# A seven-product MLP in fp32r: partial sums stay in PSUM banks that ScalarE saves and restores, split weights in one ring, and 34 of 64 half steps instead of 30 in seven products

## The chip, the core and the metric

The kernel runs on one core of one Trainium2 chip, in one launch. The metric is the device time of one execution in microseconds (us); the median of several runs is given with the lowest and the highest. Engines are named as the profile names them: PE (TensorE matmuls), PEld (its weight loads), DVE (VectorE), ACT (ScalarE), POOL (GpSimd), SP (the queue that issues the DMAs).

## What is computed

One layer of a hybrid decoder: 256 tokens, width 2048, everything in float32. An input projection feeds a state-space group and a sparse-attention group, an output projection brings both back, and an MLP follows. The change touches the MLP alone, the last two lines:

```python
    x = x + jnp.concatenate([y_ssd, y_att], axis=-1) @ w_out

    u = rmsnorm(x, g_mlp) @ w_up
    return x + jnp.square(jax.nn.relu(u)) @ w_down
```

`w_up` is 2048 x 8192 and `w_down` 8192 x 2048, 67 MB each. The "second MLP product" is the one with `w_down`.

## The kernel before

**Split numbers.** Every operand of the large products is split into a high and a low part of type fp32r: ACT casts the raw weights to the high part (L155), and DVE subtracts that from the raw weights, which leaves the low part (L156). A product of two such operands takes three matmuls (`three`, L195 to L203): high by high (L200), low by high (L202) and high by low (L203). In the MLP the row factor of the RMSNorm is left out ahead of the products. Since the ReLU is squared, it comes back as its square, `rs4`, in the additions to the residual `xr`.

**The stages.** The width 8192 of the MLP is cut into 32 pairs of 256 columns. They fall into three parts h = 0, 1, 2 of 10, 11 and 11 pairs (PARTS, L48). Each part has an up stage (`up`, L918) that makes the activations of its pairs, transposed, squared and split (`uh`, `ul`), and a down stage (`down`, L977) that multiplies them with the rows of `w_down`. A down stage has two halves, j = 0 and 1, one for each 1024 output columns. A pair in a half is called a half step here: 2 x 32 = 64 in all. PE goes through them in the order in which the code is written (PE's order is by hand, the other engines' order comes from the scheduler, which takes weights early through `high_priority`).

**A half step.** It multiplies a 2 x 2 block matrix of activations (two blocks of 128 tokens by two of 128 hidden columns) with a 2 x 2 block matrix of weights (128 rows by 512 columns each). The plain form has eight block products of `three`, 24 matmuls of 128x512. The form with seven products, in the manner of Strassen and Winograd, has seven, 21 matmuls. It needs sums of weight blocks: two additions of width 1024 (L966) and 512 (L969, two) on DVE, then casts and subtractions of the seven operands in two tiles: `wb` for three of them (L964, L974), `w2m` for the four sums (L967, L970, L974). SEVEN (L49) names the pairs in seven products: 0, 2, 4, 6, 8 in each half, 30 half steps of the 64. Below, such a half step is called S and a plain one P.

**Where sums lie.** PSUM has two sets of four banks of 128x512, tags "acc" and "mid". A half uses one set for its four output blocks (`acc`) and the other for four products of the seven that go into several output blocks (`ps7`). The other three products are added straight into `acc`. At the end of each half ACT copies the four product banks into a tile `m` (L1026), DVE combines them (L1027 to L1029), and DVE adds them (L997, through L993) and the four `acc` banks (L993) to the residual `xr`, times `rs4`. That happens in all six halves.

**Weights.** Each half step's weights, 1 MB, come with one DMA into a tile `rawm` (three of them) and are split into a `w2m` tile (three of them too). For S the sums go into `t`. So a half step's split can start as soon as a tile is free.

**CUTS (L45).** At the entry to a stage some matmuls are cut into two pieces at fixed columns (`three`, argument `cut`; the up stages have FIRST_W for it). They are the same matmuls in two pieces.

**The tail.** In the last half (h = 2, j = 1) the last two plain half steps are kept back and multiplied block by block, so that each output block of 512 columns is finished, added and stored while PE works on the next. The last block is cut into two halves of 256 columns.

## Time and profile before

| | |
|---|---|
| median of 3 runs | 1051.79 us (1051.16 to 1052.95) |
| the profiled execution, its own time | 1050.78 us |
| its span, first to last instruction | 1049.0 us |
| PE busy | 1043.5 us, 99% |
| weight loads busy | 927.1 us, 88% |
| DVE busy | 828.8 us, 79% |
| ACT busy | 565.4 us, 54% |
| granted clock of PE | 1.00 |

A row of the page gives a line of the kernel, the engine, the operation, out<-in by the program's names, the shape and how many there are; after the bar the sum of busy time and the mean of one in ns; after the second bar how long the engine stood idle just before these, and whose work ended that. A row of a timeline gives start and duration in us. Matmuls overlap, so the sum of their durations is more than the time that they take: their pace is the distance between their starts.

### The profile page before, as it was taken

The numbers are of one execution on the slowest core, as the hardware profiler recorded it, in microseconds if no ns is written. First come the engines' busy times: TensorE is split into PE (matmuls) and PEld (weight loads), VectorE is DVE, ScalarE is ACT, GpSimd is POOL, SyncE is SP. The second block draws the span as 40 slices with busy tenths as digits, with TensorE's granted clock in tenths as the row PEclk, the third lists the DMA queues.
The fourth block names the chain that finished last, engine by engine and source line by source line (L and its number), as shares of the span: only waits on it lengthen the run. The fifth ranks groups of instructions, "written<-read, shape, count | busy, mean of one in ns | idle before, by whom it ended". The sixth has DMA issues, their size and how long they took to land.

```text
span 1049.0 us, 14877 instructions
## 1 busy us (share of the span) xinstructions
PE 1043.5 (99%) x5926; PEld 927.1 (88%) x5926; DVE 828.8 (79%) x1035; ACT 565.4 (54%) x686; POOL 25.1 (2%) x30
## 2 busy tenths in 40 slices
PE   9999999999999999999999999999999999999998
PEld 8999999888888889888888898898888889888887
DVE  6698999577866557669899876688897866698996
ACT  6756555556665445445555544456545444555543
POOL 0020000122000000000000000000000000000000
PEclk9999999999999999999999999999999999999999
DMA  9957436544465536554665655555656555546671
GB/s 305 311 194 232 158 108 212 194 156 134 141 222 196 184 141 236 189 202 177 226 210 206 217 191 201 198 197 201 241 176 230 197 201 201 201 174 227 210 236 76
DMA packets 45317, 207.35 MB, mean 198 GB/s; under 512 B 4928, under 2 KB 9792, under 8 KB 29120
## 3 DMA queue, kind: packets, MB, share of 16 engines
q1 hardware_dynamic: 44960, 206.14, 57.9%
q8 instruction: 46, 0.75, 0.3%
q10 hardware_dynamic: 288, 0.26, 0.1%
q14 instruction: 23, 0.19, 0.1%
HBM read 204.29 MB, written 2.10 MB: 197 GB/s over the span
## 4 chain that ended last, share of the span: by engine, by line
PE 99%; DMA 1%; ACT 0%; DVE 0%; SPq 0%; issue 0%
PE acc L243 33%; PE acc L200 17%; PE acc L203 17%; PE acc L202 17%; PE acc L220 11%; DMA raw<-in_w_in 1%; PE ps_y L690 1%; PE ps_sr L774 0%; PE ps_l L728 0%; PE ps_o L753 0%; PE ps_s L580 0%; PE ps_s L581 0%; PE ps_dec L681 0%; PE ps_pt L745 0%; PE ps_yo L696 0%; PE pt_q L446 0%
## 5 line engine op out<-in xcount | busy, mean ns | idle before, releaser
L243 PE MATMUL acc<-x2x,w2m 128*128 128x256 f32 (+2 forms) x1987 | 331.5, 327 | 0.0
L243 PEld LDWEIGHTS acc<-x2x,w2m 128*128 128x128 f32 x1987 | 298.0, 188 | 33.2
L156 DVE TENSOR_TENSOR w2m<-rawm,w2m 128x2048 fp32r<-128x2048 f32 x96 | 219.5, 2288 | 49.2 <-ACT w2m L155 49.2
L155 ACT CAST w2m<-rawm 128x2048 fp32r<-128x2048 f32 x96 | 182.8, 1904 | 60.8 <-PE acc L203 35.6
L156 DVE TENSOR_TENSOR w<-raw,w 128x1024 fp32r<-128x1024 f32 (+1 forms) x116 | 140.2, 1214 | 71.2 <-ACT w L155 70.7
L155 ACT CAST w<-raw 128x1024 fp32r<-128x1024 f32 (+1 forms) x116 | 117.3, 1022 | 89.0 <-PE acc L203 63.6
L200 PE MATMUL acc<-w2m,uh 128*128 128x512 f32 (+3 forms) x405 | 150.2, 374 | 0.0
L203 PE MATMUL acc<-w2m,uh 128*128 128x512 f32 (+1 forms) x396 | 149.7, 378 | 0.0
L202 PE MATMUL acc<-w2m,ul 128*128 128x512 f32 (+1 forms) x396 | 149.7, 378 | 0.0
L220 PE MATMUL acc<-hx,w 128*128 128x256 f32 (+1 forms) x976 | 114.7, 278 | 0.0
L220 PEld LDWEIGHTS acc<-hx,w 128*128 128x128 f32 x976 | 112.6, 188 | 0.0
L927 ACT COPY r<-acc 128x256 f32<-128x256 f32 x64 | 23.3, 370 | 121.9 <-PE acc L243 121.3
L200 PEld LDWEIGHTS acc<-w2m,uh 128*128 128x128 f32 x405 | 76.0, 188 | 12.9
L202 PEld LDWEIGHTS acc<-w2m,ul 128*128 128x128 f32 x396 | 74.4, 188 | 12.3
L203 PEld LDWEIGHTS acc<-w2m,uh 128*128 128x128 f32 x396 | 74.3, 188 | 12.3
L967 ACT CAST w2m<-t 128x1024 fp32r<-128x1024 f32 x30 | 31.5, 1050 | 96.1 <-DVE t L966 40.7
L200 PE MATMUL acc<-w,hx 128*128 128x512 f32 (+3 forms) x226 | 82.6, 368 | 0.6 <-ACT w L356 0.6
L202 PE MATMUL acc<-w,hx 128*128 128x512 f32 (+1 forms) x222 | 79.8, 359 | 0.0
L203 PE MATMUL acc<-w,hx 128*128 128x512 f32 (+1 forms) x222 | 79.7, 359 | 0.0
L974 DVE TENSOR_TENSOR w2m<-t,w2m 128x2048 fp32r<-128x2048 f32 x30 | 68.6, 2287 | 12.7 <-ACT w2m L970 12.7
L974 DVE TENSOR_TENSOR wb<-rawm,wb 128x1536 fp32r<-128x1536 f32 x30 | 52.6, 1752 | 5.9 <-ACT wb L964 5.8
L928 DVE TENSOR_TENSOR r<-r,acc 128x256 f32<-128x256 f32 x64 | 26.4, 417 | 37.7 <-ACT r L927 37.7
(246 smaller groups left out, 1272.2 us busy)
## 6 DMA issues: line engine op xcount, KB each, us to landing
rawm<-in_w_down SPq DMA_DIRECT2D x64, 1024.0 KB, 4.8
rawm<-in_w_up SPq DMA_DIRECT2D x62, 1024.0 KB, 4.8
raw<-in_w_in SPq DMA_DIRECT2D x72, 512.0 KB, 3.9
raw<-in_w_out SPq DMA_DIRECT2D x32, 512.0 KB, 3.9
raw<-in_w_in SPq DMA_DIRECT2D x15, 256.0 KB, 5.2
raw<-in_w_in SPq DMA_DIRECT2D x16, 152.0 KB, 4.4
raw<-in_w_in SPq DMA_DIRECT2D x8, 304.0 KB, 3.3
xrow<-in_xn SPq DMA_DIRECT2D x4, 512.0 KB, 6.3
```

The lines of the kernel that those rows point to most:

```text
L155: nc.scalar.copy(hi[:, s], raw[:, s, :n])
L156: nc.vector.tensor_tensor(lo[:, s], raw[:, s, :n], hi[:, s].bitcast(F32), op=OP.subtract)
L200: nc.tensor.matmul(go(out[:, i:j]), ah, go(wh[:, i:j]), start=first and i == 0, stop=False, skip_group_check=True)
L202: nc.tensor.matmul(go(out), al, go(wh), start=False, stop=False, skip_group_check=True)
L203: nc.tensor.matmul(go(out), ah, go(wl), start=False, stop=last, skip_group_check=True)
L220: nc.tensor.matmul(acc[:, c, at:at + n], w[:, 0, s], x[:, fr:fr + n], start=(i + k + j == 0), stop=(i >= 2 and k == 7 and j == len(todo) - ...
L243: nc.tensor.matmul(walk(out[:, fr:fr + m]), w[:, k], walk(x[:, fr:fr + m]), start=(at + k + j == 0), stop=(at + k == KT - 1 and j == len(t ...
L690: nc.tensor.matmul(pt[:, 64 * i:64 * i + 64], m[i // 4][:, i % 4, :], xdt[:, c, 64 * h:64 * h + 64], start=True, stop=True)
L927: nc.scalar.copy(r[:, c], acc[:, T:])
L928: nc.vector.tensor_tensor(r[:, c], r[:, c], acc[:, :T], op=OP.add)
L967: nc.scalar.copy(ht[:, :2], t[:, :2])
L974: nc.vector.tensor_tensor(lo, x, hi.bitcast(F32), op=OP.subtract)
```

## The change

**Parts and half steps.** PARTS is (0, 11, 22, 32): parts of 11, 11 and 10 pairs. Instead of sets of pairs there is, for each half, a string of S and P (STEPS) in the order in which PE takes them; the pairs are assigned to the letters in turn, so that a pair that is S in one half is S in the other. Six S in each half of h = 0 and h = 1, five in each of h = 2: 34 half steps in seven products. The last half ends S S P P, and before it ended P S P P.

**Banks.** The sums are no longer finished at the end of each half. Between two halves ACT copies the four `ps7` banks into a tile `carry`, or the four `acc` banks into `xr`, and writes the banks' next contents into PSUM: the state of the other half's columns, from `xr` or from `carry` (`seed_acc`, `seed_p`, `save_acc`, interleaved by `exchange`). Matmuls then add to what the banks hold, without a start flag. The residual itself goes in at h = 0, multiplied by `mean2`, the inverse of `rs4`, and the factor `rs4` is applied by ACT as the bank is saved for the last time. The recombination of the four products (`solve`, `combine`) is done once for each j, in h = 2. The additions of the `acc` banks on DVE are left only in the last half.

**Weights.** The split weights of the MLP lie in one ring of 16 units of 512 columns, high parts in its first half and low parts in its second (RING). An S takes seven units, a P four, a column block of `w_up` four (it waits for five). A unit is free as soon as its last product is written down, not when the whole half step is done. The tiles `wb`, `t` and the three `w2m` are gone; the sums of weights are made in place in `rawm`. The order of the four blocks of `w_down` in memory is changed to fit that (`_quarters`). The low parts of the four sums are made in two instructions of 1024 columns where there was one of 2048, and a P that follows an S is split in two steps of two blocks (`cuts`). Where the units taken wrap around the ring's end, one more instruction is needed.

**Order.** ACT and DVE are now ordered by hand in the MLP as well: for each product on PE one step of the preparation of later weights is written down (`prepare`, as far ahead as the ring allows) and one instruction of an exchange (`lazy`).

The core of the diff:

```diff
-PARTS = (0, 10, 21, 32)
-SEVEN = (({0,2,4,6,8},{0,2,4,6,8}),({0,2,4,6,8},{0,2,4,6,8}),({0,2,4,6,8},{0,2,4,6,8}))
+PARTS = (0, 11, 22, 32)
+STEPS = (("SPSPSSPSSPP", "PSSPSPSSPSP"), ("SPSPSSPSSPP", "PSSPSPSSPSP"), ("SPSSPSPSPP", "PSSPSPSSPP"))
+TAGS = (("mid", "acc"), ("acc", "mid"), ("mid", "acc"))
+UP = ("acc", "mid", "acc")
+RING = 16
 
 A11, A21, A12, A22 = range(4)
 S1, S2, S4 = 4, 5, 6
-S3 = {7: 1, 8: 7}
-E, G, P1, F, M6 = range(5)
+S3 = 1
+P1, M6, E, F = range(4)
...
+    ring = mlp.tile([P, 2 * RING * 512 + SPARE], F32R, name="w2m")
...
+    def take(n):
+
+        if wide[0]:
+            wide[0] = False
+            head[0] += 1
+        units = [(head[0] + i) % RING for i in range(n)]
+        while any(busy[q] for q in units):
+            yield False
+        for q in units:
+            busy[q] = True
+        head[0] = (head[0] + n) % RING
+        return units
...
+    def plain(src, cuts):
+
+        with tc.high_priority(offset=HP):
+            raw = load(src, 512)
+        units = yield from take(4)
+        n = 4 // cuts
+        for i in range(0, 4, n):
+            with tc.high_priority(offset=HP):
+                for hi, lo, x in view(units[i:i + n], raw[:, i:i + n]):
+                    nc.scalar.copy(hi, x)
+                    nc.vector.tensor_tensor(lo, x, hi.bitcast(F32), op=OP.subtract)
+            if i + n < 4:
+                yield True
+        w22, w11, w21, w12 = (part(q) for q in units)
         return [[w11, w12], [w21, w22]]
...
-    def seven(src, behind):
+    def seven(src):
 
...
+            raw = load(src, 512)
+        own = yield from take(3)
+        with tc.high_priority(offset=HP):
+            for hi, lo, x in view(own, raw):
+                nc.scalar.copy(hi, x)
+                nc.vector.tensor_tensor(lo, x, hi.bitcast(F32), op=OP.subtract)
+        yield True
+        sums = yield from take(4)
+        outer, inner = (list(view(sums[2 * i:2 * i + 2], x)) for i, x in enumerate((raw[:, ::3], raw[:, 1:3])))
+        with tc.high_priority(offset=HP):
+            nc.vector.tensor_tensor(raw[:, ::3], raw[:, :2], raw[:, 3:].to_broadcast([P, 2, 512]), op=OP.add)
+            for hi, lo, x in outer:
+                nc.scalar.copy(hi, x)
+        yield True
+        with tc.high_priority(offset=HP):
+            for i in range(1, 3):
+                nc.vector.tensor_tensor(raw[:, i], raw[:, i], raw[:, i - 1], op=OP.add)
+            for hi, lo, x in outer:
+                nc.vector.tensor_tensor(lo, x, hi.bitcast(F32), op=OP.subtract)
+            for hi, lo, x in inner:
+                nc.scalar.copy(hi, x)
+        yield True
+        with tc.high_priority(offset=HP):
+            for hi, lo, x in inner:
+                nc.vector.tensor_tensor(lo, x, hi.bitcast(F32), op=OP.subtract)
+        return [part(own[i]) for i in (1, 2, 0)] + [part(sums[i]) for i in (1, 0, 2, 3)]
...
+    def seed_acc(h, j, i):
+
+        b, c = divmod(i, 2)
+        t = accumulator(TAGS[h][j])
+        state.setdefault((h, j), [[], []])[0].append(t)
+        src = xr[:, b, 1024 * j + 512 * c:1024 * j + 512 * c + 512]
+        if (h, j) == (2, 1):
+            return
+        if h:
+            nc.scalar.copy(t, src)
+        else:
+            nc.scalar.activation(t, src, AF.Copy, scale=mean2[:, b:b + 1])
+
+    def seed_p(h, j, i):
+
+        state.setdefault((h, j), [[], []])
+        t = accumulator(TAGS[h][1 - j])
+        state[h, j][1].append(t)
+        if h:
+            nc.scalar.copy(t, carry[:, 4 * j + (P1, F, E, M6)[i]])
+
+    def save_acc(h, j, i):
+
+        b, c = divmod(i, 2)
+        dst = xr[:, b, 1024 * j + 512 * c:1024 * j + 512 * c + 512]
+        if h + j == 2:
+            nc.scalar.activation(dst, state[h, j][0][i], AF.Copy, scale=rs4[:, b:b + 1])
+        else:
+            nc.scalar.copy(dst, state[h, j][0][i])
...
+        if g == 5:
+            for i in range(4):
+                seed_acc(h, 0, i)
...
+    def exchange(saves, seeds):
+
+        for i in range(5):
+            lazy.extend(saves[i:i + 1] + seeds[i - 1:i] if i else saves[:1])
...
+    def down_body(h, j, t, w):
+
...
+        if marked:
+            b11, b21, b22, t1, t3, t2, t4 = w
+            first = t == min(i for i, s in enumerate(steps) if s[1])
+            done = t == max(i for i, s in enumerate(steps) if s[1])
+            new = first and not h
+            p1, p5, p7, p6 = ps7
+            for n, (to, slot, right) in enumerate(((acc[0], A12, b21), (acc[1], S4, b22), (acc[2], A22, t4), (p1, A11, b11),
+                                                   (p5, S1, t1), (p7, S3, t3), (p6, S2, t2))):
+                go(to, x, slot, right, new if n > 2 else n not in opened, done and n > 2)
+                opened.add(n)
+                free(right[2])
+                if done and n == 6:
+                    exchange([lambda i=i: nc.scalar.copy(carry[:, 4 * j + (P1, F, E, M6)[i]], ps7[i]) for i in range(4)],
+                             [lambda i=i: seed_acc(h, 1, i) for i in range(4)] if j == 0 else [])
+                    if h == 2:
+                        solve(j)
...
+            turn = [(2 * b + c, k) for k in range(2) for c in range(2) for b in range(NB)]
+            for i, k in sorted(turn) if final else turn:
+                b, c = divmod(i, 2)
+                go(acc[i], x, 2 * k + b, w[k][c], i not in opened, final and k == 1)
+                opened.add(i)
+                if b:
+                    free(w[k][c][2])
+                if final and (i, k) == (3, 1):
+                    exchange([lambda i=i: save_acc(h, j, i) for i in range(4)],
+                             [lambda i=i: seed_p(h, 1, i) for i in range(4)] if j == 0 else [])
+                    if (h, j) == (2, 0):
+                        combine(0)
+                        lazy.append(lambda: [nc.sync.dma_start(out[b * P:(b + 1) * P, :1024], xr[:, b, :1024])
+                                             for b in range(NB)])
+                yield
...
+    for h in range(3):
+        for g in range(PARTS[h + 1] - PARTS[h]):
+            tag = "mid" if (h, g) in ((0, 1), (0, 3)) else UP[h]
+            for c in range(2) if h + g else ():
+                todo.append((lambda g=g, h=h, c=c: up_weights(w_up[PARTS[h] + g][c]),
+                             lambda w, h=h, g=g, c=c, tag=tag: up_body(h, g, c, w, accumulator(tag))))
+        for j in range(2):
+            for t, (g, marked) in enumerate(order[h, j]):
+                src = w_down[j, PARTS[h] + g]
+                cuts = 2 if t and order[h, j][t - 1][1] else 1
+                todo.append((lambda src=src, marked=marked, cuts=cuts: seven(src) if marked else plain(src, cuts),
+                             lambda w, h=h, j=j, t=t: down_body(h, j, t, w)))
...
+                    moved = next(task)
+                except StopIteration as e:
+                    ready.append(e.value)
+                    break
+                if not moved:
+                    yield
...
+    with tc.manual_schedule(engines={nc.scalar.engine, nc.vector.engine}):
+        prep = prepare()
+        next(prep, None)
+        for c in range(2):
+            up_rest(0, 0, c, first[c])
+        for i, (_, body) in enumerate(todo):
+            for _ in body(ready[i]):
+                if lazy:
+                    lazy.pop(0)()
+                next(prep, None)
...
-    w = np.stack([w[:, k, :, :, c] for k, c in ((0, 1), (0, 0), (1, 0), (1, 1))], axis=3)
+    w = np.stack([w[:, k, :, :, c] for k, c in ((1, 1), (0, 0), (1, 0), (0, 1))], axis=3)
```

Two places in the order of the instructions. First DVE in the first half of the down stage h = 0, before. `wb` and `w2m` are split weights, `t` sums of weights, `rawm` weights as they were loaded:

```order
L974 TENSOR_TENSOR wb<-rawm,wb 128x1536
L966 TENSOR_TENSOR t<-rawm 128x1024
L156 TENSOR_TENSOR w2m<-rawm,w2m 128x2048
L969 TENSOR_TENSOR t<-t,rawm 128x512 x2
L974 TENSOR_TENSOR w2m<-t,w2m 128x2048
L974 TENSOR_TENSOR wb<-rawm,wb 128x1536
L966 TENSOR_TENSOR t<-rawm 128x1024
L156 TENSOR_TENSOR w2m<-rawm,w2m 128x2048
```

The piece holds S, P, S and the beginning of the next: a P (one L156) stands between the first sum (L966) of an S and its second sums (L969). The same engine in the same half, after:

```order
L998 TENSOR_TENSOR w2m<-rawm,w2m 128x1024 x2
L1012 TENSOR_TENSOR w2m<-rawm,w2m 128x1536
L1017 TENSOR_TENSOR rawm<-rawm 128x2x512
L1023 TENSOR_TENSOR rawm<-rawm 128x512 x2
L1025 TENSOR_TENSOR w2m<-rawm,w2m 128x1024
L1031 TENSOR_TENSOR w2m<-rawm,w2m 128x1024
L1012 TENSOR_TENSOR w2m<-rawm,w2m 128x1536
L1017 TENSOR_TENSOR rawm<-rawm 128x2x512
L1023 TENSOR_TENSOR rawm<-rawm 128x512 x2
L1025 TENSOR_TENSOR w2m<-rawm,w2m 128x1024
L1031 TENSOR_TENSOR w2m<-rawm,w2m 128x1024
L998 TENSOR_TENSOR w2m<-rawm,w2m 128x1024 x2
```

Here two S follow each other (L1012 to L1031, twice), each with six instructions for its sums and splits, and a P cut in two (L998 x2) stands ahead and behind: P S S P, where S and P took turns.

Second ACT at the end of a half, where the banks are copied. Before, after the first half of h = 1 (`m` is the tile for the recombination, `acc` a bank):

```order
L964 CAST wb<-rawm 128x1536
L1026 COPY m<-acc 128x512 x3
L967 CAST w2m<-t 128x1024
L1026 COPY m<-acc 128x512
L970 CAST w2m<-t 128x1024
L155 CAST w2m<-rawm 128x2048
L967 CAST w2m<-t 128x1024
```

Four copies stand between the casts of weights. After, between the two halves of h = 1 (`carry` and `xr` hold banks, and copies whose output is `acc` write a bank):

```order
L1200 COPY carry<-acc 128x512
L1011 CAST w2m<-rawm 128x1536
L1200 COPY carry<-acc 128x512
L1046 COPY acc<-xr 128x512
L1200 COPY carry<-acc 128x512
L1046 COPY acc<-xr 128x512
L1200 COPY carry<-acc 128x512
L1046 COPY acc<-xr 128x512 x2
L1019 CAST w2m<-rawm 128x1024
L1027 CAST w2m<-rawm 128x1024
L1065 COPY xr<-acc 128x512
L1011 CAST w2m<-rawm 128x1536
```

Four banks are saved and four are written, one each in turn, and only one cast (L1011) stands among these eight; the next pair of casts (L1019, L1027) comes behind them.

More of the change, by code (lines that the diff above doesn't have):

```diff
@@ L31 @@
 RB = 5
-WIDE_B = 3
 WIDE_R = 3
@@ L947, in plain @@
-    def plain(src):
-        hi, lo = operands(src, 512, shift=SHIFT, parts=4)
-        w12, w11, w21, w22 = ((hi[:, i], lo[:, i]) for i in range(4))
+    carry = units.tile([P, 8, 512], F32, name="carry")
+    half = [slice(0, 512), slice(512, 1024)]
+    order = {}
+    for h in range(3):
+        own = [[i for i, s in enumerate(STEPS[h][0]) if s == c] for c in "SP"]
+        for j in range(2):
+            left = [list(o) for o in own]
+            order[h, j] = [(left["SP".index(s)].pop(0), s == "S") for s in STEPS[h][j]]
@@ new lines, in hymba_kernel, with go @@
+    cut = {}
+    count = [0]
+    kept = []
+    opened = set()
+    def go(out, left, slot, w, first, last=False):
+        three(out, left[0][:, slot], left[1][:, slot], *w[:2], first, last, cut.get(count[0]))
+        count[0] += 1
+    def down_body(h, j, t, w):
+        steps = order[h, j]
+        g, marked = steps[t]
+        x = u[h, g]
+        end = (h, j) == (2, 1)
+        final = t == len(steps) - 1
+        if t == 0 or marked and len(state[h, j][1]) < 4:
+            flush()
+        if t == 0:
+            cut.clear()
+            if interrupted("down"):
+                cut.update(CUTS)
+            count[0] = 0
+            opened.clear()
+            if not end:
+                opened.update(range(4))
+        acc, ps7 = state[h, j]
+        if marked:
[14 more added lines that the diff above has]
+                        solve(j)
+                        if end:
+                            combine(j)
+                yield
+        elif end and t >= len(steps) - 2:
+            kept.append((x, w))
+            if final:
+                flush()
+                finale(acc)
+        else:
+            turn = [(2 * b + c, k) for k in range(2) for c in range(2) for b in range(NB)]
[12 more added lines that the diff above has]
+                                             for b in range(NB)])
+                yield
+        if final:
+            other.append("down")
@@ L1070, in down @@
-            add(1, slice(768, 1024), rest, True)
-    for h, (tag, tags) in enumerate((("acc", ("mid", "acc")), ("mid", ("acc", "mid")), ("acc", ("mid", "acc")))):
-        down(h, up(h, tag), tags)
+                    go(acc[i], left, 2 * k + b, w[k][c], False, left is kept[-1][0] and k == 1)
+            add(b, 1, half[c], acc[i], True)
+        c = slice(0, 256)
+        for left, w in kept:
+            for k in range(2):
+                go(acc[3][:, c], left, 2 * k + 1, [x[:, c] for x in w[k][1][:2]], False, left is kept[-1][0] and k == 1)
```

282 lines of the change are left out of this document (140 added, 142 removed).

## The prediction

> **What bounds the kernel now.** I read the page first: the busy times, then the chain that ended last.
>
> ```profile
> span 1049.0 us, 14877 instructions
> PE 1043.5 (99%) x5926; PEld 927.1 (88%) x5926; DVE 828.8 (79%) x1035; ACT 565.4 (54%) x686; POOL 25.1 (2%) x30
> PE 99%; DMA 1%; ACT 0%; DVE 0%; SPq 0%; issue 0%
> ```
>
> PE is busy for all but 5.5 us, and the chain is PE from end to end. That leaves two questions: does PE wait anywhere, and how fast do its matmuls follow each other? The waits of PE alone:
>
> ```profile
> PE ps_w L258 <- POOL ones L253: 1.3, 1, 1.3
> PE acc L200 <- ACT w L356: 0.6, 1, 0.6
> ```
>
> Both lie in the first microseconds; the MLP has none. Next the windows: before the MLP, the MLP, the tail, and of the three down stages (h = 0, 1, 2) the first (columns: length, then busy time and count of PE, PEld, DVE, ACT, POOL, then clock, DMA share, GB/s).
>
> ```profile
> 387.00:1045.50 658.50, 658.43 (x3510) 578.28 (x3508) 541.77 (x495) 340.72 (x314) 0.00 (x0) 1.00 0.59 203
> 1045.50:1049.00 3.50, 0.00 (x0) 0.00 (x0) 0.46 (x1) 0.00 (x0) 0.00 (x0) 1.00 0.19 68
> ```
> ```profile
> 491.12:590.44 99.32, 99.32 (x458) 84.88 (x456) 90.00 (x69) 56.79 (x49) 0.00 (x0) 1.00 0.62 212
> ```
>
> The clock is 1.00 throughout. In the down stage PE has no gap, but DVE is close behind: 90.0 of 99.3 us. A matmul's own duration says little, since matmuls overlap, so I take the distance of starts. Three stretches of the timeline, PE alone: the first down stage, and two places in the output projection before the MLP.
>
> ```profile
> 535.65 0.38 PE L200 MATMUL acc<-w2m,uh 128*128 128x512 f32 x1
> ...
> 547.97 0.38 PE L203 MATMUL acc<-w2m,uh 128*128 128x512 f32 x1
> ```
> ```profile
> 347.49 0.39 PE L200 MATMUL acc<-w,yah 128*128 128x512 f32 x1
> ...
> 349.50 0.38 PE L200 MATMUL acc<-w,yah 128*128 128x512 f32 x1
> ```
> ```profile
> 297.69 0.39 PE L200 MATMUL acc<-w,yah 128*128 128x512 f32 x1
> ...
> 303.86 0.39 PE L200 MATMUL acc<-w,yah 128*128 128x512 f32 x1
> ```
>
> In the first, 56 matmuls lie between the two starts: 12.32/56 = 0.2200 us each. In the second 9: 2.01/9 = 0.2233. In the third 27: 6.17/27 = 0.2285. The same shape at the same clock has at least three paces, though PE waits for nobody in any of them; the down stages run at the best. So a gain can come only from fewer matmuls, and a loss from a wait or from a worse pace.
>
> **The matmuls removed.** A half step in seven products has 7 x 3 = 21 matmuls of 512 columns, a plain one 8 x 3 = 24. With 34 instead of 30 in seven products, 4 x 3 = 12 fall away; up stages, split pieces and the last half steps keep their number. 12 x 0.2200 = 2.64 us, all on the path.
>
> The Trainium skill, page "TensorE: Matmul & The Clock Gate", section "Back-to-back issue gap", gives about 131 ns per 512-column matmul as the sustained rate of a LDWEIGHTS and matmul stream. By it the sum would be 1.57 us, an estimate. No stretch above comes near it.
>
> **The splitting of weights on DVE.** Groups of the MLP's DVE instructions by shape, then those of ACT (mean ns after the comma):
>
> ```profile
> L156 DVE TENSOR_TENSOR w2m<-rawm,w2m 128x2048 fp32r<-128x2048 f32 x96 | 219.5, 2288 | 49.2 <-ACT w2m L155 49.2
> L974 DVE TENSOR_TENSOR w2m<-t,w2m 128x2048 fp32r<-128x2048 f32 x30 | 68.6, 2287 | 12.7 <-ACT w2m L970 12.7
> L974 DVE TENSOR_TENSOR wb<-rawm,wb 128x1536 fp32r<-128x1536 f32 x30 | 52.6, 1752 | 5.9 <-ACT wb L964 5.8
> L969 DVE TENSOR_TENSOR t<-t,rawm 128x512 f32<-128x512 f32 x60 | 41.1, 685 | 0.7
> L966 DVE TENSOR_TENSOR t<-rawm 128x1024 f32<-128x1024 f32 x30 | 36.5, 1217 | 4.2 <-DMA rawm<-in_w_down 4.1
> L993 DVE SCALAR_TENSOR_TENSOR xr<-acc,rs,xr 128x512 f32<-128x512 f32 x23 | 15.8, 742 | 0.8 <-PE acc L203 0.8
> L993 DVE SCALAR_TENSOR_TENSOR xr<-m,rs,xr 128x1024 f32<-128x1024 f32 x12 | 15.2, 1277 | 0.0
> L1029 DVE TENSOR_TENSOR m<-m 128x1024 f32<-128x1024 f32 x6 | 7.3, 1221 | 0.1
> L1028 DVE TENSOR_TENSOR m<-m 128x512 f32<-128x512 f32 x6 | 4.1, 690 | 0.1
> L1027 DVE TENSOR_TENSOR m<-m 128x512 f32<-128x512 f32 x6 | 4.1, 684 | 1.0 <-ACT m L1026 1.0
> ```
> ```profile
> L155 ACT CAST w2m<-rawm 128x2048 fp32r<-128x2048 f32 x96 | 182.8, 1904 | 60.8 <-PE acc L203 35.6 <-PE acc L243 24.5 <-DMA rawm<-in_w_up 0.6
> L967 ACT CAST w2m<-t 128x1024 fp32r<-128x1024 f32 x30 | 31.5, 1050 | 96.1 <-DVE t L966 40.7 <-PE acc L203 33.3 <-DVE t L969 10.5
> L1026 ACT COPY m<-acc 128x512 f32<-128x512 f32 x24 | 13.5, 589 | 2.6 <-PE acc L203 2.2
> L942 ACT CAST uh<-r 128x512 fp32r<-128x512 f32 x17 | 10.6, 622 | 0.7 <-DVE r L929 0.7
> ```
>
> Call a half step in seven products S, a plain one P. DVE's work for an S was 1.217 + 2 x 0.685 + 1.752 + 2.287 = 6.63 us. Now the low parts of the sums come in two pieces of 1024: 1.217 + 2 x 0.685 + 1.752 + 2 x 1.217 = 6.77. A P costs 2.29, or 2 x 1.217 = 2.43 where it is cut in two. Removed: 5 halves x 4 adds x 0.742 = 14.8 us, and in four halves the recombination, 4 x (0.684 + 0.690 + 1.221 + 2 x 1.277) = 20.6: together 35.4. Added: four P that become S, 4 x (6.77 - 2.29) = 17.9, 30 x 0.14 = 4.2 and 23 cut P x 0.14 = 3.2: 25.3. Summed over the MLP DVE loses 10 us. It is not on the path, so this is worth nothing as a sum, and what counts is where the rest lies.
>
> Before, S and P took turns: DVE 6.63 + 2.29 = 8.92 us against PE's 45 x 0.22 = 9.90. Now come groups S S P: DVE 2 x 6.77 + 2.43 = 15.97, PE 66 x 0.22 = 14.52. By mean durations DVE falls 1.45 us behind in each. But neighbouring DVE instructions overlap: in the rows of the tail below, one starts at 1026.84 and takes 2.29, and the next starts at 1029.04, 0.09 before its end. With 18 instructions per group that is 1.6 us, and the group comes out even. Five of the six halves have two such groups, in two of them back to back; the sixth has one.
>
> How late may DVE be? The ring has 16 units and an S takes 7. The second S of a pair can write its two last units only when the P before the pair is done with them; its third product reads one of them. Between lie 21 + 6 matmuls and a bit, about 6 us. In them stand an ACT cast (1.05) and two DVE subtractions (2 x 1.22): some 2.5 us are left for a backlog, against 0 to 2.9 from two groups. I expect no wait in most halves and 0.1 us in all.
>
> **The tail.** DVE before, from the timeline, and PE's last split matmuls:
>
> ```profile
> 1026.84 2.29 DVE L974 TENSOR_TENSOR w2m<-t,w2m 128x2048 fp32r<-128x2048 f32 x1
> 1029.04 2.28 DVE L156 TENSOR_TENSOR w2m<-rawm,w2m 128x2048 fp32r<-128x2048 f32 x1
> 1032.08 2.29 DVE L156 TENSOR_TENSOR w2m<-rawm,w2m 128x2048 fp32r<-128x2048 f32 x1 [0.76 <-ACT w2m L155]
> ...
> 1038.05 2.48 DVE L993 SCALAR_TENSOR_TENSOR xr<-m,rs,xr 128x1024 f32<-128x1024 f32 x2
> 1040.45 1.40 DVE L993 SCALAR_TENSOR_TENSOR xr<-acc,rs,xr 128x512 f32<-128x512 f32 x2
> ...
> 1045.47 0.48 DVE L993 SCALAR_TENSOR_TENSOR xr<-acc,rs,xr 128x256 f32<-128x256 f32 x1 [0.54 <-PE acc L203]
> ```
> ```profile
> 1042.45 0.28 PE L200 MATMUL acc<-w2m,uh 128*128 128x256 f32 x1
> ```
>
> The last weights were ready at 1032.08 + 2.29 = 1034.37. The closing block starts 36 matmuls before 1042.45, at 1034.53, and reads their low part in its ninth, at 1036.3: 1.9 us to spare. The last half now ends S S P P, not P S P P: DVE gets 6.77 - 2.43 = 4.3 us more, PE 0.66 less, 5.0 together. DVE idled 0.76 before its last subtraction and now and then earlier. Between all of the 5.0 covered and 1.9 + 0.76 covered, PE waits 0 to 2.3 us; nearer to the first, since the recombination after it has 1045.47 - 1040.53 = 4.9 us of cover. I take 0.2.
>
> **ACT.** 56 copies of 512 are new: 20 saves of plain banks, 36 that write a bank. A save is a row above, 0.589. No row of ACT writes a bank: the nearest are 0.589 (out of a bank) and 0.622 (SBUF to SBUF); I take 0.62. That is 20 x 0.589 + 36 x 0.62 = 34 us of an engine with 340.7 of 658.5 in use. Eight copies (5 us) stand at each exchange, behind them the casts of the next weights; the other set of banks, with a P or two (5.3 us each), covers them. Uncovered, PE would wait up to 0.6 per copy. I cost this at nothing.
>
> **The sum.** 2.64 - 0.1 - 0.2 = 2.34 us off the profiled execution's 1050.78 (its span and 1.78 around it): 1048.4. The median shown is 1051.79, 1.01 above; from it 1049.45, say **1049.4**.
>
> **The rivals.**
> - *DVE late.* The groups S S P cost their 1.45 us here and there, and the tail up to 2.3: 0.8 to 2.6 us of the gain go, leaving 1049.9 to 1051.8. For it: DVE at 90 of 99 us. Against it: before, DVE was busy without a break for whole stretches and PE never waited. 1050.8.
> - *The pace is lost* (the slower side). Something disturbs PE's rhythm at the entry to a down stage, a wait or another order, and 1434 matmuls run at 0.2233 or 0.2285: 4.7 to 12.2 us lost, 1053.9 to 1061.4; I take the nearer row, 1054. It turns slower by 0.2% from a mean of 0.2233 on. For it: the paces exist. Against it: the split pieces at the entry (CUTS) and the shapes that follow are the same.
> - *A removed matmul is worth only 0.13 us*: 12 x 0.131 = 1.6, 1050.2. Against it: every row above.
>
> **How the numbers follow.** A measurement here tells about 0.2% (2.1 us) from no change; that is 1049.69. My forecast has 0.58, of which 0.06 fall short of that bound, since it clears it by 0.3 us only; DVE late 0.30; the pace lost 0.10; the cheap matmul 0.02. Faster 0.52, same 0.38, slower 0.10. The range takes the full 2.64 off the profiled execution itself at the low end, 1050.78 - 2.64 = 1048.1, and all of DVE late at the high end, 1051.8; outside lie the lost pace and a rest.
>
> **What would show it.** Right: PE's starts 0.2200 apart in the down stages, stages 108.2, 108.2 and some 99 us long, no PE wait above 0.3 us. DVE late: PE waits for DVE's low parts at the second S of a pair or for the last P. The pace lost: PE busy throughout and a distance of 0.2233 or more. The forecast is wrong if the time lies above 1049.7 without any of these.

## The result, and the profile after

| | time | lowest to highest |
|---|---|---|
| before | 1051.97 us | 1051.16 to 1052.95, 6 runs |
| changed | 1059.86 us | 1056.02 to 1061.55, 6 runs |

The ratio is 1.007, with a 95% interval from 1.0052 to 1.0088: slower, where 1049.4 was forecast. The profiled execution took 1060.54. The page, the chain that ended last and the waits of PE:

```profile
span 1058.5 us, 15127 instructions
PE 1052.7 (99%) x5914; PEld 926.3 (88%) x5914; DVE 831.2 (79%) x1087; ACT 604.6 (57%) x785; POOL 25.1 (2%) x30
PE 93%; DVE 4%; ACT 2%; issue 1%; POOL 0%; ACTq 0%; DVEq 0%; POOLq 0%
```
```profile
PE acc L199 <- DVE w2m L1031: 0.8, 2, 0.5
PE acc L196 <- ACT w2m L1027: 0.2, 1, 0.2
```

PE is still 99% busy, with 12 matmuls fewer, and the new waits sum up to 1.0 us. Yet the span is 9.5 us longer. So the loss is in matmuls whose starts lie further apart. Windows of the changed kernel (columns as in the prediction): down stage h = 0, down stage h = 1, up stage h = 2, down stage h = 2; then of the kernel before, its down stage h = 1 and the up stage after it.

```profile
502.43:614.11 111.68, 111.40 (x500) 92.56 (x498) 100.46 (x91) 67.90 (x75) 0.00 (x0) 1.00 0.58 210
...
731.55:842.41 110.86, 110.15 (x499) 92.48 (x498) 100.16 (x92) 71.03 (x82) 0.00 (x0) 1.00 0.58 215
842.41:952.04 109.63, 109.63 (x643) 96.91 (x642) 76.09 (x78) 57.70 (x61) 0.00 (x0) 1.00 0.52 188
952.04:1054.68 102.64, 102.64 (x469) 85.14 (x467) 95.01 (x90) 58.52 (x65) 0.00 (x0) 1.00 0.50 187
```
```profile
707.89:817.76 109.87, 109.87 (x505) 93.89 (x504) 96.63 (x73) 60.31 (x50) 0.00 (x0) 1.00 0.62 211
817.76:935.22 117.46, 117.46 (x707) 105.70 (x705) 87.77 (x89) 56.58 (x55) 0.00 (x0) 1.00 0.57 197
```

Counted in matmuls of 512 columns (pieces and halves added up), the old stage h = 1 has 498 in 109.87 us, and the changed stages h = 0 and 1 have 492: six fewer, so 109.87 - 6 x 0.22 = 108.55 was to be had. They took 3.13 and 2.31 us more. The last down stage has 450, as the first one before, which took 99.32: 3.32 more. The up stage h = 2 has 480 where the old one has 528, so 117.46 x 480/528 = 106.78 was to be had: 2.85 more, and there is no wait in it. Together 11.6 us; less the 2.64 that the 12 matmuls brought, 9.0. The rest lies ahead of the MLP, whose first up stage begins 0.6 us later.

The timeline of PE at the first wait, in the second S of the second pair in the first half of h = 0 (L198 is low by high, L199 high by low, L196 high by high), then two starts further on in that stage:

```profile
543.00 0.38 PE L196 MATMUL acc<-w2m,uh 128*128 128x512 f32 x1
543.22 0.39 PE L198 MATMUL acc<-w2m,ul 128*128 128x512 f32 x1
543.89 0.50 PE L199 MATMUL acc<-w2m,uh 128*128 128x512 f32 x1 [0.28 <-DVE w2m L1031]
544.23 0.39 PE L196 MATMUL acc<-w2m,uh 128*128 128x512 f32 x1
...
559.99 0.39 PE L196 MATMUL acc<-w2m,uh 128*128 128x512 f32 x1
...
572.32 0.39 PE L196 MATMUL acc<-w2m,uh 128*128 128x512 f32 x1
```

Ahead of the wait the starts are 0.22 apart. The matmul that waits for a low part comes 0.45 us late, and the one after it another 0.12: 0.57 us in all. That is small. But then 54 matmuls take 12.33 us, 0.2283 each, and it stays so to the end of the stage: some 306 matmuls x 0.0083 = 2.5 us. The wait costs its own length and, four times as much, the pace behind it. In h = 1 PE waits at the same half step, and in h = 2 in the first pair S S:

```profile
771.90 0.39 PE L199 MATMUL acc<-w2m,uh 128*128 128x512 f32 x1
772.47 0.50 PE L196 MATMUL acc<-w2m,uh 128*128 128x512 f32 x1 [0.18 <-ACT w2m L1027]
772.80 0.39 PE L198 MATMUL acc<-w2m,ul 128*128 128x512 f32 x1
773.73 0.49 PE L199 MATMUL acc<-w2m,uh 128*128 128x512 f32 x1 [0.54 <-DVE w2m L1031]
774.06 0.39 PE L196 MATMUL acc<-w2m,uh 128*128 128x512 f32 x1
...
968.43 0.39 PE L198 MATMUL acc<-w2m,ul 128*128 128x512 f32 x1
968.75 0.49 PE L199 MATMUL acc<-w2m,uh 128*128 128x512 f32 x1
969.08 0.38 PE L196 MATMUL acc<-w2m,uh 128*128 128x512 f32 x1
```

By the same count, start to start less 0.22 for each, 2.16 - 0.88 = 1.28 us and 0.65 - 0.44 = 0.21 us. The third is so short that the list of waits has no line for it (PE had no idle time there; the start is merely late), and the pace is lost all the same: "no wait" below means none that the list names. All waits make 2.06 us of the 11.6, the pace 9.5. Behind the wait in h = 1 the pace is 0.2233, behind the two others 0.2283.

Why DVE was late is in its own timeline, in the stretch that leads to the first wait:

```profile
527.66 2.35 DVE L998 TENSOR_TENSOR w2m<-rawm,w2m 128x1024 fp32r<-128x1024 f32 x2
529.93 1.75 DVE L1012 TENSOR_TENSOR w2m<-rawm,w2m 128x1536 fp32r<-128x1536 f32 x1
531.71 1.22 DVE L1017 TENSOR_TENSOR rawm<-rawm 128x1024 f32<-128x1024 f32 x1
532.97 1.42 DVE L1023 TENSOR_TENSOR rawm<-rawm 128x512 f32<-128x512 f32 x2
534.30 1.22 DVE L1025 TENSOR_TENSOR w2m<-rawm,w2m 128x1024 fp32r<-128x1024 f32 x1
535.58 1.23 DVE L1031 TENSOR_TENSOR w2m<-rawm,w2m 128x1024 fp32r<-128x1024 f32 x1
536.95 1.76 DVE L1012 TENSOR_TENSOR w2m<-rawm,w2m 128x1536 fp32r<-128x1536 f32 x1
...
543.76 1.22 DVE L998 TENSOR_TENSOR w2m<-rawm,w2m 128x1024 fp32r<-128x1024 f32 x1
```

One P and two S, from 527.66 to 543.76, take 16.10 us; PE needs 66 x 0.22 = 14.52 for them. DVE idles no more than 0.14 us at a time there (ahead of 536.95) and falls 1.58 us behind in each group. That fits h = 0 and 1, where the wait comes in the second of two groups. In h = 2 the first pair is late already. There DVE had idled 0.75 us at the beginning of the stage, for a cast of ACT (L1011, at 950.99) that runs right behind two of the new copies into banks (L1056, 949.95 to 951.06). So the copies may have a part in the third wait; no run separates the two.

### The profile page after: what moved, and what is told of

Read it like the earlier page. It is cut to its first block, busy times and chain, and to the rows that moved or that the text cites. A ratio compares the mean times of both kernels' runs of the same rounds, so it can differ in the third digit from the quotient of the medians.

```text
span 1058.5 us, 15127 instructions
## 1 busy us (share of the span) xinstructions
PE 1052.7 (99%) x5914; PEld 926.3 (88%) x5914; DVE 831.2 (79%) x1087; ACT 604.6 (57%) x785; POOL 25.1 (2%) x30
## 4 chain that ended last, share of the span: by engine, by line
PE 93%; DVE 4%; ACT 2%; issue 1%; POOL 0%; ACTq 0%; DVEq 0%; POOLq 0%
PE acc L1079 31%; PE acc L199 15%; PE acc L196 15%; PE acc L198 15%; PE acc L216 11%; DVE w2m L1012 1%; DVE rawm L1023 1%; PE acc L237 1%; DVE rawm L1017 1%; PE ps_y L684 1%; ACT w2m L1011 1%; ACT w2m L1027 1%; PE ps_sr L768 0%; PE ps_l L722 0%; PE ps_o L747 0%
## 5 line engine op out<-in xcount | busy, mean ns | idle before, releaser
L199 PE MATMUL acc<-w2m,uh 128*128 128x512 f32 (+1 forms) x482 | 185.1, 384 | 0.8 <-DVE w2m L1031 0.8
L196 PE MATMUL acc<-w2m,uh 128*128 128x512 f32 (+5 forms) x497 | 185.4, 378 | 0.2 <-ACT w2m L1027 0.2
L198 PE MATMUL acc<-w2m,ul 128*128 128x512 f32 (+1 forms) x482 | 184.8, 383 | 0.0
L985 DVE TENSOR_TENSOR w2m<-rawm,w2m 128x2048 fp32r<-128x2048 f32 x62 | 141.9, 2289 | 46.1 <-ACT w2m L984 45.8
L984 ACT CAST w2m<-rawm 128x2048 fp32r<-128x2048 f32 x62 | 118.0, 1904 | 9.0 <-issue 2.9
L196 PEld LDWEIGHTS acc<-w2m,uh 128*128 128x128 f32 x497 | 92.9, 187 | 18.6 <-ACT w2m L1027 0.6
L199 PEld LDWEIGHTS acc<-w2m,uh 128*128 128x128 f32 x482 | 90.4, 187 | 19.1 <-DVE w2m L1031 2.0
L198 PEld LDWEIGHTS acc<-w2m,ul 128*128 128x128 f32 x482 | 90.4, 188 | 17.3
L1019 ACT CAST w2m<-rawm 128x1024 fp32r<-128x1024 f32 (+1 forms) x35 | 35.8, 1025 | 87.2 <-DVE rawm L1017 80.4
L196 PE MATMUL acc<-w,hx 128*128 128x512 f32 (+3 forms) x226 | 82.5, 368 | 0.0
L198 PE MATMUL acc<-w,hx 128*128 128x512 f32 (+1 forms) x222 | 79.7, 359 | 0.0
L199 PE MATMUL acc<-w,hx 128*128 128x512 f32 (+1 forms) x222 | 79.7, 359 | 0.0
L998 DVE TENSOR_TENSOR w2m<-rawm,w2m 128x1024 fp32r<-128x1024 f32 (+3 forms) x59 | 70.7, 1237 | 6.3 <-ACT w2m L997 6.3
L1012 DVE TENSOR_TENSOR w2m<-rawm,w2m 128x1536 fp32r<-128x1536 f32 (+2 forms) x37 | 59.8, 1624 | 6.9 <-ACT w2m L1011 6.4
L997 ACT CAST w2m<-rawm 128x1024 fp32r<-128x1024 f32 (+3 forms) x59 | 59.4, 1059 | 7.1 <-DMA rawm<-in_w_down 7.0
```

The lines of the kernel that those rows point to most:

```text
L196: nc.tensor.matmul(go(out[:, i:j]), ah, go(wh[:, i:j]), start=first and i == 0, stop=False, skip_group_check=True)
L198: nc.tensor.matmul(go(out), al, go(wh), start=False, stop=False, skip_group_check=True)
L199: nc.tensor.matmul(go(out), ah, go(wl), start=False, stop=last, skip_group_check=True)
L984: nc.scalar.copy(hi, raw)
L985: nc.vector.tensor_tensor(lo, raw, hi.bitcast(F32), op=OP.subtract)
L997: nc.scalar.copy(hi, x)
```

## The experiments

Three theories. **A**: DVE falls behind in the groups S S P, PE waits briefly, and the break in its rhythm costs the pace until cut pieces restore it. **B**: the pace is lost by the new way of keeping sums and weights (banks written by ACT, the ring). **C**: the waits themselves are the loss. Each experiment was timed beside the kernel before on its own chip, so medians are compared within a pair. The ratio and its interval stand beside them as the record has them; the ratio need not be the quotient of the two medians.

**1. S and P in turn.** The changed kernel with other strings:

```diff
+STEPS = (("SPSPSPSPSPP", "PSPSPSPSPSP"), ("SPSPSPSPSPP", "PSPSPSPSPSP"), ("SPSPSPSPPP", "PSPSPSPSPP"))
```

> The changed kernel with other strings: S and P alternate nowhere S S (SPSPSPSPSPP and PSPSPSPSPSP in h = 0 and 1, SPSPSPSPPP and PSPSPSPSPP in h = 2), 28 half steps in seven products; ring, bank exchanges and recombination as in the change. Theory A (DVE falls behind in the groups S S P, PE waits briefly, and each wait throws its matmuls out of the pace of 0.2200 us until the next stage): no wait of PE in the down stages, 0.2200 from start to start throughout, and 6 x 0.2200 = 1.3 us more than before: 1053.3. Theory B (the pace is lost because ScalarE reads and writes PSUM banks between halves, or by where the ring's weights lie, whatever DVE does): 0.2233 or more as in the changed kernel, 18 matmuls more than it has, 1059.9 + 4.0 = 1063.8. Theory C (the waits themselves are the loss): no waits, but as A, 1053.3.

Measured: 1053.64 against 1052.46 before, ratio 1.0002 (0.9986 to 1.0019). No wait in the MLP. Its windows, down stages h = 0 and 1, then up stage h = 2:

```profile
503.19:613.06 109.87, 109.87 (x505) 93.89 (x504) 92.02 (x82) 65.47 (x72) 0.00 (x0) 1.00 0.58 218
...
730.51:840.39 109.88, 109.88 (x506) 93.89 (x505) 91.84 (x83) 68.69 (x78) 0.00 (x0) 1.00 0.58 217
840.39:947.17 106.78, 106.78 (x642) 96.10 (x641) 74.92 (x75) 56.87 (x61) 0.00 (x0) 1.00 0.52 191
```

These down stages have 498 matmuls each, like the old stage of 109.87 us, and take exactly as long. Saving and writing the banks, the ring and the order by hand cost PE nothing. That is against B.

**2. Two sums on GpSimd.** The same 34 S, with the two last sums of each S taken off DVE:

```diff
-                nc.vector.tensor_tensor(raw[:, i], raw[:, i], raw[:, i - 1], op=OP.add)
+                nc.gpsimd.tensor_tensor(raw[:, i], raw[:, i], raw[:, i - 1], op=OP.add)
```

> The changed kernel, but the two last sums of weights of each S (512 columns each, 1.42 us of DVE together) are made by GpSimd. All 34 S, the strings and the exchanges stay. Theory A: DVE gains 2.8 us on each group S S P, which is more than the 1.45 us by which it fell behind; no wait in the down stages, pace 0.2200, 1049.3 to 1050.0, unless GpSimd's additions take over 2.5 us for the pair. Theory B: the pace is lost as before, 1058 to 1061. Theory C: as A for the waits, so only about 2 us better than the changed kernel if the slower pace stays.

Measured: 1125.7, ratio 1.0686 (1.0664 to 1.0707). PE's longest wait, and GpSimd's group:

```profile
PE acc L196 <- ACT w2m L1027: 31.3, 11, 4.8
```
```profile
L1023 POOL TENSOR_TENSOR rawm<-rawm 128x512 f32<-128x512 f32 x68 | 115.5, 1698 | 729.5 <-DVE rawm L1017 659.8 <-issue 67.0
```

The pair takes 3.4 us and not 1.42, so that the case kept open in the expectation came: casts and low parts stand behind the additions on ACT and DVE. The granted clock was lower too, 0.95 to 0.96 in the down stages. The experiment tells nothing about A and B. The Trainium skill, page "Trainium Architecture — The Big Picture", section "The five engines, in one table", gives GpSimd as 2x slower than DVE in streaming elementwise work; here it is 1698 ns to 692 (L1023 in the changed kernel), 2.5 times.

**3. The pieces once more.** The changed kernel, with the entry's cut pieces set again behind the last pair S S of each first half:

```diff
+        if j == 0 and t == (4 if h == 2 else 9):
+            cut.update({count[0] + i: c for i, c in CUTS.items()})
```

> The changed kernel, and the cut pieces that stand at the entry to each down stage (CUTS) are set once more in the first half of each part, in the P behind the last pair S S. The waits stay. Theory A: from these pieces on PE runs at 0.2200 again, in each of the three down stages and in the up stage of h = 2, unless it waits again: the waits' 2 us and some of the pace remain, 1051.5 to 1054. Theory B: the pace is lost again soon after the pieces without a wait, 1057 to 1061. Theory C: no change, 1059.9.

Measured: 1053.76 against 1052.46, ratio 1.0015 (1.0005 to 1.0025). In the timeline of h = 0 the same wait, the first new piece (x2) and the pace behind the last one:

```profile
543.48 0.50 PE L199 MATMUL acc<-w2m,uh 128*128 128x512 f32 x1 [0.29 <-DVE w2m L1031]
543.81 0.38 PE L196 MATMUL acc<-w2m,uh 128*128 128x512 f32 x1
...
546.32 0.39 PE L199 MATMUL acc<-w2m,uh 128*128 128x512 f32 x1
546.55 0.39 PE L196 MATMUL acc<-w2m,uh 128*128 128x320 f32 x2
...
552.25 0.38 PE L198 MATMUL acc<-w2m,ul 128*128 128x512 f32 x1
...
553.57 0.38 PE L198 MATMUL acc<-w2m,ul 128*128 128x512 f32 x1
```

Behind the wait 2.51/11 = 0.228, behind the pieces 1.32/6 = 0.220. The wait is still there, and yet the kernel is 1.3 us over the one before, where the changed one is 7.9 over it (5.6 in experiment 10). The stages h = 0 and 1 took 109.48 and 110.15 us, and the up stage h = 2 106.78. In the last half of h = 2 PE waits again, and there A's rule has an exception:

```profile
1008.73 0.49 PE L199 MATMUL acc<-w2m,uh 128*128 128x512 f32 x1 [0.29 <-DVE w2m L1031]
...
1009.51 0.38 PE L199 MATMUL acc<-w2m,uh 128*128 128x512 f32 x1
...
1018.75 0.38 PE L199 MATMUL acc<-w2m,uh 128*128 128x512 f32 x1
```

The wait makes 0.58 us by the count above, as long as the one in h = 0. But behind it 42 matmuls take 9.24 us, 0.2200 each, and no piece stands between.

**4. A late DVE in the kernel before.** Nothing of the change; two subtractions of one S are made twice:

```diff
-                w = seven(w, g - 1 in marked) if g in marked else plain(w)
+                w = seven(w, g - 1 in marked, (h, j, g) == (0, 0, 4)) if g in marked else plain(w)
...
-                nc.vector.tensor_tensor(lo, x, hi.bitcast(F32), op=OP.subtract)
+                for _ in range(LATE if late else 1):
+                    nc.vector.tensor_tensor(lo, x, hi.bitcast(F32), op=OP.subtract)
```

> The kernel before with one thing added: in the first half of h = 0, the two subtractions of the split of pair 4 are made twice (4.0 us of DVE, the second time with the same result). No banks are written, no ring. Theory A: DVE's delay leaves PE waiting once or twice, 0 to 3.7 us, and from then on to the next up stage, some 250 to 350 matmuls, the pace is 0.2233 to 0.2285: another 0.8 to 3.0 us on top of the waits. Theory B: the waits alone, pace 0.2200 behind them. Theory C: the waits alone.

Measured: 1055.02 against 1052.46, ratio 1.0034 (1.0019 to 1.005). The stage took 101.99 us where it had 99.32. Three late starts, two of them waits that the list names, make 0.67 + 0.21 + 0.69 = 1.57 us of the 2.67; the other 1.1 is a pace of 0.2233 between them. A's sum holds without any of the change. Four of the 12 runs took 1058.8 to 1060.07, and the profiled one, 1059.78, is of these: there the pace was lost a second time, in h = 1, at a matmul that starts 0.08 us late with no wait named, and the up stage behind it took 120.56 us where it had 117.46.

**5. The fourth sum last.** Same S, same strings; in the second S of a pair the product that waited comes last:

```diff
+            if t and steps[t - 1][1]:
+                todo.append(todo.pop(2))
```

> The changed kernel with the same 34 S and the same strings; in the second S of each pair the product with the fourth sum of weights, third of seven before, comes last. That is 4 products or 2.6 us later on PE for the operand for which PE waited. Nothing is taken off DVE, ACT or the banks. Theory A (brief waits for DVE break the pace): the waits in the first halves go, the pace stays 0.2200 in h = 0 and h = 1; the last half (S S P P at the end) may still wait 0.5 to 2.5 us. 1050.0 to 1052.5. Theory C (the waits are the loss): the waits' 2 us come back and the slower pace stays, 1057 to 1058. No more than 0.2% off the changed kernel would refute A.

Measured: 1056.79 against 1053.43, ratio 1.003 (1.0014 to 1.0045). A's number was missed. By the bar that the expectation set, a gain of no more than 0.2% over the changed kernel, the time does not settle it either: against the 1.007 of that kernel's first ratio the gain is 0.4%, against the 1.0045 of experiment 10 it is 0.15%. What speaks for A is the trace. The DVE waits of the first halves are gone and the pace of 0.2200 holds to the end of these halves. But then PE is late for the next one in line: 0.2 us in h = 0 and 0.4 in h = 1 at the exchange of banks, and 1.3 us for the last weights in the tail. Behind the break in h = 0 the up stage took 120.57 us.

```profile
PE acc L199 <- DVE w2m L998: 1.3, 1, 1.3
```

**6. And the tail.** As 5, and the closing block takes the first kept half step for all three full blocks ahead of the second:

```diff
-        for i in (0, 2, 1):
-            b, c = divmod(i, 2)
-            for left, w in kept:
+        for left, w in kept:
+            for i in (0, 2, 1):
+                b, c = divmod(i, 2)
```

> As the one with the fourth sum last, and in the tail the first kept plain half step is multiplied with all three full blocks before the second kept one (12 matmuls or 2.6 us more for the last weights). Theory A: no wait above 0.3 us in any down stage, 0.2200 throughout: 12 x 0.2200 = 2.6 us under the kernel before, 1049.3 to 1050. Theory C: 1057.

Measured: 1054.67 against 1053.43, ratio 1.0001 (0.9988 to 1.0014). A's number, 1049.3 to 1050, and C's 1057 were both missed. No wait for DVE in the MLP is left in the list. One for ACT is, where a bank of the next half is written (h = 1):

```profile
783.18 0.39 PE L199 MATMUL acc<-w2m,uh 128*128 128x512 f32 x1
784.05 0.50 PE L196 MATMUL acc<-w2m,uh 128*128 128x512 f32 x1 [0.48 <-ACT acc L1046]
```

That is 0.76 us by the count above. Behind it the pace is 0.2233, and the up stage that follows takes 109.63 us again and not 106.78. In h = 0 the pace breaks at the same exchange (at 556.3) with no wait named, and that stage took 109.39 us.

**7. And the pieces.** As 6, with the edit of 3.

> As the one with the fourth sum last and the tail in another order, with the cut pieces set again in the P behind the last pair S S of each first half. Theory A: where no wait is left the pieces only cost their own time, 3 x some 0.25 us, 1050 to 1051; where a wait is left in a run, its loss of pace ends at the pieces, and the runs spread less. Theory C: no difference to the one without pieces.

Measured: 1054.61 against 1053.43, ratio 1.0005 (0.9991 to 1.0019). A's number (1050 to 1051) was missed, and the spread did not shrink (1051.48 to 1057.48): the waits that are left, in h = 1 and 2, come behind the pieces.

**8. One cut in the kernel before.** No wait, no work:

```diff
-CUTS = {0: 320, 5: 144, 8: 160, 13: 160, 16: 160}
+CUTS = {0: 320, 5: 144, 8: 160, 13: 160, 16: 160, 45: 256}
```

> The kernel before, and in the first half of each down stage one more matmul, of product 45, is cut into two pieces of 256 columns: three extra instructions in all, no work and no wait is added. Theory A, in the form that any break of PE's rhythm costs the pace, a wait or not: behind each cut some 330 matmuls at 0.2233 to 0.2285, 3 x 1.1 to 2.8 us: 1055 to 1060. Theory A in the form that it takes a wait: 3 x 0.05 us, 1052. Theory C: 1052.

Measured: 1054.96 against 1053.43, ratio 1.0011 (1.0002 to 1.0021). The timeline at the cut and further on, and the window of that stage:

```profile
522.20 0.39 PE L200 MATMUL acc<-wb,uh 128*128 128x256 f32 x2
522.43 0.39 PE L202 MATMUL acc<-wb,ul 128*128 128x512 f32 x1
...
560.19 0.38 PE L203 MATMUL acc<-w2m,uh 128*128 128x512 f32 x1
...
571.58 0.39 PE L203 MATMUL acc<-w2m,uh 128*128 128x512 f32 x1
```
```profile
492.19:592.57 100.38, 100.38 (x458) 84.80 (x457) 90.08 (x69) 56.87 (x49) 0.00 (x0) 1.00 0.61 210
```

The cut itself costs 0.01 us. Behind it 51 matmuls take 11.39 us, 0.2233 each, and the stage 1.06 us more; the other two stages take 111.11 and 111.13 us, 1.2 more. PE waited for nothing. So it does not take a wait: a matmul cut at another column is enough. C has no place for that. B neither, since this is the kernel before. In the trace the three stages lose 3.5 us together, while the medians lie 1.5 apart. The kernel before spreads over 6.4 us on this chip; its slower executions may lose the pace too, but only one execution of it has a profile.

**9 and 10. No waits, and the changed kernel again, on one chip.** As 6, with the fourth sum last in every S but the first of a half, and with the banks of a half's first half step taken one after the other:

```diff
-            if t and steps[t - 1][1]:
+            if t > 1:
                 todo.append(todo.pop(2))
...
-            for i, k in sorted(turn) if final else turn:
+            for i, k in sorted(turn) if final or not t else turn:
```

> As the one with the fourth sum last and the tail in another order, with two more moves of PE's order: the product with the fourth sum comes last in every S but the first of a half, and the first half step of a half goes through its four banks one after the other (two products each) where it changed banks at every product, so that the banks that ScalarE writes are needed 0, 1.3, 2.6 and 4.0 us after the first. Still 34 S, no work taken off any engine. Theory A (any break of PE's rhythm, mostly a wait, costs the pace until the next pieces): no wait in the down stages, stages of 108.5, 108.5 and 99.5 us, 2.3 to 2.6 us under the kernel before on the same chip. Theory C (the waits alone are the loss): no better than the one with the tail in another order, whose profile has 0.7 us of waits left: at most 0.7 us better.

> The changed kernel once more, on the chip of the one without waits, so that the two can be compared. Theory A: waits at the same places as in its first profile (second S of the second pair in the first halves of h = 0 and 1, of the first pair in h = 2), 7 to 9 us over the one without waits. Theory C: 2 us over it.

Measured: 1053.14 (1050.88 to 1057.34) without waits, 1058.58 for the changed kernel, 1052.97 before; ratios to before 0.9997 (0.9979 to 1.0016) and 1.0045 (1.0029 to 1.0061). The down stages of the one without waits:

```profile
503.99:612.81 108.82, 108.82 (x500) 92.73 (x498) 98.80 (x92) 66.48 (x72) 0.00 (x0) 1.00 0.58 212
...
730.26:839.75 109.49, 109.49 (x500) 92.60 (x498) 99.61 (x92) 70.13 (x80) 0.00 (x0) 1.00 0.58 215
...
946.53:1046.79 100.26, 100.09 (x469) 85.17 (x467) 94.36 (x89) 58.04 (x65) 0.00 (x0) 1.00 0.51 188
```

The first is 0.3 us over what was to be had, the second and third 0.9 each. In the first the pace breaks late in the stage with no wait that the profile names; in the second PE is 0.2 us late at the exchange of banks, and the pace behind is lost. In the third it is 0.44 and 0.26 us late for two sums of the last group; behind the first of these the pace is 0.2200 again after seven matmuls, behind the second it is 0.2233. 5.4 us lie between the two kernels, under A's 7 to 9, but nearer to it than to C's 2. The 2.3 us under the kernel before that A expected are not shown. The changed kernel had its waits at the same places as in its first profile, and in the last half three short ones more (0.19 to 0.39 us).

**11. The kernel before without pieces.**

```diff
-CUTS = {0: 320, 5: 144, 8: 160, 13: 160, 16: 160}
+CUTS = {}
```

> The kernel before without the cut pieces at the entry to its down stages (CUTS is empty); 15 matmul instructions fewer, the same work, no wait added. Theory A, with the pace as a state that only the pieces set to 0.2200: the three down stages run at the pace with which they begin, 0.2233 to 0.2285 (the rows of the first stage before its pieces show 0.2277), 1446 x 0.0033 to 0.0085 = 4.8 to 12.3 us more, 1057 to 1065, less 0.7 us for the pieces' own time. Theory B (the pace depends on where weights and banks lie): 0.2200 as before, 1051 to 1052.

Measured: 1055.51 against 1052.08, ratio 1.0034 (1.0022 to 1.0047). The first down stage:

```profile
491.51:592.07 100.56, 100.56 (x452) 84.32 (x451) 90.31 (x69) 56.85 (x49) 0.00 (x0) 1.00 0.60 209
```

1.24 us more in the first stage, and 1.4 in each of the others (111.28 and 111.31): 0.2233, the nearer of the two paces. The time is below the range in the expectation, but by its mechanism. In the down stages the 0.2200 is what the pieces bring.

## Why the prediction was wrong

- **PE bounds the kernel, and a loss can only come from a wait or a worse pace.** Right. PE is 99% busy before and after, and the whole loss is in starts that lie further apart.
- **12 matmuls at 0.2200.** Right as a price: experiment 1 has the new program at the old pace, stage for stage, and the first down stage of experiment 9 took 1.05 us less than the old one with 498, where six matmuls are worth 1.32. No version brought the whole 2.64 in. With the 0.131 us of the Trainium skill's page "TensorE: Matmul & The Clock Gate", section "Back-to-back issue gap", nothing here agrees: no stage came under 0.2200. The same section's formula for a single matmul, 512/2.4 + 2.5 ns, gives an estimate of 0.216, which is near.
- **The group S S P on DVE "comes out even".** This is the step that failed first. By mean durations I had 15.97 us and set 1.6 us of overlap against it, taken from one pair of neighbours in the tail and multiplied by 18 instructions. The rows show 14 instructions in a group, so that even by this rule 0.2 us were left. And they show 16.10 us: four neighbours overlap, by 0.08 or 0.09, and seven others leave gaps of 0.03 to 0.14, mostly where an instruction works on what the one just ahead of it wrote, or waits for a cast. DVE falls 1.58 us behind per group, not zero. Two groups make 3.2 us, the room that I had worked out was 2.5, and PE waited 0.6 us and 1.3 us in h = 0 and 1. So the room was about right there; it does not explain the 0.2 us in h = 2. With the duration that I had, and without the overlap, the first two waits were to be seen.
- **A wait is priced at its length.** This is the step that cost most. The sum took "0.1 us in all" for the waits, and the rival "DVE late" took 0.8 to 2.6 us, both as if PE went on behind a wait as before. The waits were 2.06 us, and the slower pace behind them 9.5: alone it turns the gain of 2.64 into a loss.
- **DVE loses 10 us over the MLP.** It was busy for 2 us more: 544.06 us over the six stages, where it had 541.77. The adds and recombinations went as costed. But two more pairs in seven products also need two more sets of activation sums (some 2.8 us by the groups of the up stages), which I had left out, and overlaps between neighbours went from 21.9 us to 16.2, added up over the rows. Some 4 us stay unexplained. As said there, the sum decides nothing.
- **The tail, 0 to 2.3 us.** In the changed kernel's first profile nothing, since PE was behind already, and 0.2 us in that of experiment 10. In experiment 5, at the better pace, PE waited 1.3 us there: inside the bounds, far from the 0.2 that I took.
- **ACT's 56 copies at nothing.** In the changed kernel no wait of PE is put down to them, though two of them stand ahead of the cast that made DVE idle in h = 2. A copy into a bank took 0.59 or 0.60 us (0.62 taken), and 0.69 where it applies a factor. When DVE's waits were taken away, the exchange was the next in line (0.76 us in experiment 6): the cover that I named has no room to spare.
- **The rival "pace lost"**, with 1053.9 to 1061.4 and a chance of 0.10, is what happened, from 1056.02 to 1061.55. Its size was right and its place was wrong, so the agreement of the two ranges is in part luck: I looked for a disturbance at the entry, where the pieces stand, and all 1434 matmuls at a slower pace. The breaks came in the middle of the stages, and some of the loss in an up stage. It also stood beside "DVE late" as a case of its own, while the one is what brings the other about. DVE late by 0.2 to 1.3 us is to be priced at that plus, in most cases, 0.0033 to 0.0083 us for every matmul that is left in the stage. With that the 0.30 for DVE late would have stood on the slower side.
- **The up stages.** The working has no loss in them, and the 1434 matmuls of the rival "pace lost" are those of the down stages alone. In h = 2 the loss was 2.85 us: a slower pace can go past the end of the down stage.

What stays open: why PE has these paces, and why a break ends in 0.2233 one time, in 0.2283 another and now and then in 0.2200 again. The runs show what starts a slower pace and what ends it, not what it is. Also open is what 34 S are worth without any break, since a version without one was not reached: the best runs of experiment 9 took 1050.88 us, and of the kernel before on that chip 1050.94. None of the versions beats the kernel before.

## What to carry to other kernels

In a kernel that PE bounds, read the distance of matmul starts stage by stage, ahead of and behind each wait: a short wait can cost several times its length in what follows. An engine that hides behind PE is to be costed in the longest run of its heavy steps, start to start and without overlap, and its lateness compared with the room that the buffers leave; the sum over the kernel says nothing. When one late operand is mended, the next one in line shows, so look for it before the change is judged.

## What the runs showed of the hardware

- A matmul of 128x512 at a granted clock of 1.00 follows the one before it at 0.2200, 0.2233 or 0.2283 us, in stretches of up to hundreds. One matmul cut at column 256 ended the first of them in all three stages of experiment 8; pieces at other columns bring it back (experiment 3). A late start mostly ends it too: leaving out experiment 2, PE came 0.17 us or more late some 20 times while its starts in a down stage were 0.2200 apart, and in all but two cases the pace behind was a slower one. The two are at 1008.73 in experiment 3 and at 1033.42 in experiment 9.
- The kernels at the better pace spread more. With the cut of experiment 8, at 0.2233, 12 runs lay within 0.9 us (1054.49 to 1055.41), and without the pieces of experiment 11 nine of ten within 1.2, the tenth 2.6 above them; the kernel before on the chip of experiment 8 spread over 6.4 (1051.22 to 1057.58). That the pace is lost now and then in the latter is likely, but not shown.
- The up stage after a down stage took 2.7% more in some runs with no wait in it (109.63 for 106.78 us, 120.56 for 117.46). In all profiles this came only behind a down stage that ended at 0.2233, 5 times of 14, and never behind one that ended at 0.2200 or 0.2283. At 0.2233 the starts lie 0.222 and 0.225 apart in turn. In these five the first matmul of the up stage came 0.227 or 0.228 behind the last of the down stage, in the other nine 0.221 or 0.222.
- An addition of 128x512 in float32 took 1.70 us on GpSimd (experiment 2) and 0.69 on DVE (the changed kernel).
